# A transformer block in split fp32: the gt2 loads queued behind the up phase's high parts, and the squares of the transposed x1 taken ahead of its copy

## The chip, the cores and the metric

The kernel runs on one core of a Trainium2 chip. The metric is the time of one execution in device microseconds (us); lower is better. TensorE (PE) multiplies, PEld is its weight load, VectorE (DVE) and ScalarE (ACT) work elementwise, GpSimd (POOL) here mostly issues DMAs that add in DRAM, and SyncE (SP) issues most of the other DMAs. ACT issues DMAs too: the gt2 loads stand in its own instruction queue.

## The reference

One layer, 512 tokens, model width 2048, all in fp32. What matters here, shortened:

```python
mod = silu(c) @ w_ada + b_ada                      # (1, 6 * 2048)
sh1, sc1, gt1, sh2, sc2, gt2 = split(mod, 6)
h   = rms_norm(x, g_mix) * (1 + sc1) + sh1
mix = both head groups of h                        # recurrent and attention
x1  = x + gt1 * (mix @ w_out)
h2  = rms_norm(x1, g_ffn) * (1 + sc2) + sh2
gate, up = split(h2 @ w_up, 2)                     # 2 x 5632 columns
out = x1 + gt2 * ((silu(gate) * up) @ w_down)
```

## The kernel before

Activations lie transposed: features on the 128 partitions, 512 tokens along the row. Each fp32 operand of a matmul is split into a high part (ACT rounds a copy, `wsplit` L227) and a low part (DVE subtracts, L228), and a product is three matmuls: high by high, high by low, low by high. A framework schedules: each engine gets one queue in order, worked out at build time from priorities (`tc.high_priority(offset=...)` lifts a block) and from what depends on what. `tc.issue_after(ins)` makes every instruction of its block stand behind `ins`, if both are on the same engine. A tile pool with a tag and `bufs=n` is a ring of n buffers; a new tile waits until every reader of the old one is done.

The stages, in order: the first projections and the heads (to about 585 us), the output projection (`wo0` to `wo3`, four groups of 512 columns, 16 steps of 128 input features each), two groups of the up projection in the plain way (`up0`, `up1`), then 40 groups `uf4` to `uf43` of the up projection by a scheme of seven products of half blocks (the up phase), then the down projection in four phases (`dn`).

The six gates of `mod` are dot products of `silu(c)` with rows of `w_ada`. Five of them are computed along the way as `ada` tiles, loaded by SP. The last, gt2, is cut into 64 pieces of 128 by 512: `gt2_load(n)` loads piece n on ACT's queue into one of two buffers, `gt2_piece(n)` starts load n + 1 and has DVE multiply and sum piece n (L182). The program calls the pieces one for each chunk of the up phase, from chunk 16 on. The products end in `mods[GT2]` (`mod5`); `gt2_spread` stores it transposed to DRAM (`gt2d`, 4-byte elements, L1144) and reads it back as rows that the down projection needs at its end.

The x1 of each output group is also wanted by tokens: `x1_by_tokens(a)` has PE transpose four tiles of 128 by 128 into each of four PSUM banks, ACT copies each bank into a page in SBUF (tag "d", four pages), squares that copy into a second page with the row sums in `ss1`, and SP stores the copy as `x1t`. The banks of group a are those which group a + 2's sums take next, and `ss1` is the input of `rstd_1`, from which the up projection's operands are made (`make_t`). It is called at step 13 of the next group (`X_STEPS`), for the last group at step 6 of `up0`, and `rstd_1` is spread at step 10.

In the up phase each chunk's weights (2048 columns) give four split blocks: a, c, s and t (`uq25_1sl` is group 25, chunk 1, block s, low). The last stage's tiles are `dq4_0tl` (activations of product 4, part 0) and `dq4_0w0h` (its weights). In the profile's names such numbers are mostly left out.

Of the kernel before, what the change touches and what calls it, by code (L numbers as in the profile page):

```python
# [10 lines left out]
AF = mybir.ActivationFunctionType  # L11
# [5 lines left out]
S = 512  # L17
KT = D // P
# [13 lines left out]
SH1, SC1, GT1, SH2, SC2, GT2 = range(6)  # L32
# [27 lines left out]
def R(ap):  # L60
    return ap.bitcast(F32R)
# [3 lines left out]
def block_kernel(ctx, tc, xT, crow, adaT, vecs, bfr, w1, wyr, wqkv0, wqkv, wgate, wout, wup0, wups, wdn, outT):  # L65
    nc = tc.nc
# [15 lines left out]
    def page(name, tag, shape=None):  # L82
        return pgp.tile(shape or [P, S], F32, tag=tag, name=name, bufs=TAGS[tag])
# [85 lines left out]

    def gt2_load(n):  # L170
        t = cp.tile([P, S], F32, name=f"gt2_{n}", tag="ssq", bufs=2)
        nc.scalar.dma_start(out=t, in_=adaT[GT2 * KT + n // 4, :, (n % 4) * S:(n % 4 + 1) * S])
        gt2_src[n] = t

    def gt2_piece(n):
        if n == 0:
            gt2_load(0)
        if n < 4 * KT - 1:
            gt2_load(n + 1)
        t = gt2_src.pop(n)  # L180
        r = n % 4
        nc.vector.scalar_tensor_tensor(out=t, in0=t, scalar=1.0, in1=c_b[:, r * S:(r + 1) * S], op0=ALU.mult, op1=ALU.mult,  # L182
                                       accum_out=gt2_acc[:, r, n // 4:n // 4 + 1])
        if n == 4 * KT - 1:
            m = mods[GT2]
            nc.vector.tensor_add(m, gt2_acc[:, 0, :], vec[:, V_BADA + GT2 * KT:V_BADA + (GT2 + 1) * KT])
            for r in range(1, 4):
                nc.vector.tensor_add(m, m, gt2_acc[:, r, :])
# [4 lines left out]

    pending = []

    tail_lo = []

    def ada_some(n, ahead=True):
        with tc.issue_after(tail_lo[-1]):
# [24 lines left out]
    def wsplit(raw_ap, n, name):  # L224
        hi = wp.tile([P, 1024], F32, tag="whi", name=name + "h")
        lo = wp.tile([P, 1024], F32, tag="wlo", name=name + "l")
        nc.scalar.activation(R(hi[:, :n]), raw_ap, AF.Copy)  # L227
        tail_lo.append(nc.vector.tensor_sub(R(lo[:, :n]), raw_ap, hi[:, :n]).ins)  # L228
        return hi, lo

# [3 lines left out]
    def stream(src, kts, width, name, raw_hook=None, ahead=AHEAD):  # L234
        for q in range(len(kts) // 4):
            with tc.high_priority(offset=ahead):
                raw = wp.tile([P, 2048], F32, tag="raw", name=f"{name}r{q}", bufs=RAW)
                nc.sync.dma_start(out=raw[:, :4 * width], in_=src[kts[q * 4] // 4])
            if raw_hook:
                raw_hook(q, raw)  # L240
            for hf in range(2):
                with tc.high_priority(offset=ahead):
                    hi, lo = wsplit(raw[:, hf * 2 * width:(hf + 1) * 2 * width], 2 * width, f"{name}{q}_{hf}")
                for k2 in range(2):
                    yield kts[q * 4 + hf * 2 + k2], hi[:, k2 * width:(k2 + 1) * width], lo[:, k2 * width:(k2 + 1) * width]
# [118 lines left out]
    for kt in range(KT):  # L364
# [5 lines left out]
        a = cp.tile([P, 1], F32, name=f"A{kt}")  # L370
# [21 lines left out]
    for f in (4, 5, 6, 7, 0, 1, 2, 3):  # L392
        t = page(f"xr{f}", "c")
# [35 lines left out]
    for f in range(4):  # L429
        t = page(f"yr{f}", "c")  # L430
# [369 lines left out]
    for f in range(4):  # L800
        g, w = yr1[f], page(f"ge{4 + f}", "c")
# [23 lines left out]
    def bank(i, f, name):  # L825
        return acc(name) if i % 2 == 0 else (misc(name) if f < 3 else rgp(name))
# [20 lines left out]
    ss1 = cp.tile([P, NT, 4], F32, name="ss1")  # L847
# [3 lines left out]
    def x1_by_tokens(a):  # L851
        for t in range(NT):
            pt = bank(a + 1, t, f"x1p{a}_{t}")
            for k in range(4):
                nc.tensor.transpose(out=pt[:, k * P:(k + 1) * P], in_=x1[4 * a + k][:, t * P:(t + 1) * P], identity=ident)
            w, sq = page(f"x1w{a}_{t}", "d"), page(f"x1s{a}_{t}", "d")
            with tc.high_priority(offset=EVAC):
                nc.scalar.activation(w, pt, AF.Copy)
            nc.scalar.activation(sq, w, AF.Square, accum_out=ss1[:, t, a:a + 1])
            x1t[t, a] = drp.tile([P, S], F32, name=f"x1t{a}_{t}")  # L860
            nc.sync.dma_start(out=x1t[t, a], in_=w)
    late = []
# [5 lines left out]
    for g in range(4):  # L868
# [8 lines left out]
        if g:  # L877
            add(hk, X_STEPS[g - 1], lambda a=g - 1: x1_by_tokens(a))
        late = []
        ps = fm_group(wout[g], korder, mix, f"wo{g}", hooks=hk, ps=[bank(g + 1, f, f"wo{g}p{f}") for f in range(4)])  # L880
        for f in range(4):
            kt = g * 4 + f
            t = page(f"x1_{kt}", "c")
# [140 lines left out]
    def fast_chunk(f, c):  # L1024

        nm = f"uq{f}_{c}"
        with tc.high_priority(offset=AHEAD):
            if c:
                raw = bp.tile([P, 2048], F32, tag="raw2", name=nm + "r")
            else:  # L1030
                raw = wp.tile([P, 2048], F32, tag="raw", name=nm + "r", bufs=RAW)
            for i in range(2):
                ld = nc.sync.dma_start(out=raw[:, i * 1024:(i + 1) * 1024], in_=wups[f - 2 * STD, c, :, i * 1024:(i + 1) * 1024])
            up_loads.append(ld.ins)
            blocks = raw.rearrange("p (b m) -> p b m", b=4)
            hi, lo = wsplit(raw[:, :1024], 1024, nm + "a")
            out = [(4, hi[:, :512], lo[:, :512]), (1, hi[:, 512:], lo[:, 512:])]
            hi, lo = page(nm + "ch", "d"), page(nm + "cl", "d")
            nc.scalar.activation(R(hi), blocks[:, 3], AF.Copy)
            nc.vector.tensor_sub(R(lo), blocks[:, 3], hi)  # L1040
            out.append((2, hi, lo))
            nc.vector.tensor_add(blocks[:, 0:3:2], blocks[:, 0:2], blocks[:, 2:3].broadcast_to([P, 2, 512]))  # L1042
            nc.vector.tensor_add(blocks[:, 1], blocks[:, 1], blocks[:, 0])  # L1043
            hi, lo = wsplit(raw[:, :1024], 1024, nm + "s")
            out += [(5, hi[:, :512], lo[:, :512]), (6, hi[:, 512:], lo[:, 512:])]
            nc.vector.tensor_add(blocks[:, 3], blocks[:, 3], blocks[:, 1])  # L1046
            hi, lo = wsplit(raw[:, 1024:], 1024, nm + "t")
            out += [(7, hi[:, :512], lo[:, :512]), (3, hi[:, 512:], lo[:, 512:])]
        return out
# [5 lines left out]
    for f in range(2 * STD, FT):  # L1055
        ps = [bank(f + 1, b, f"uf{f}p{b}") for b in range(4)]
        m = {p: ps[b][:, h * HS:(h + 1) * HS] for p, (b, h) in where.items()}
        for c in range(2):
# [10 lines left out]
            n = 2 * (f - 2 * STD) + c  # L1069
# [28 lines left out]
    def dn_chunk(ph, q, hold=False):  # L1098
        prods = PHASES[ph]
        out = {p: [] for p, _, _ in prods}  # L1100
        with tc.high_priority(offset=AHEAD):
            raws, ts = [], []
            for n, (p, blk, ix) in enumerate(prods):
                nm = f"dq{p}_{q}"
                raws.append(dn_load("raw2" if n or (len(prods) == 1 and q % 2) else "raw", blk, q, nm + "r"))
                tl, th = page(nm + "tl", "h"), page(nm + "th", "h")
                nc.sync.dma_start(out=tl, in_=td[ph][q][:, ix])
                nc.scalar.activation(R(th), tl, AF.Copy)
                nc.vector.tensor_sub(R(tl), tl, th)
                ts.append((th, tl))  # L1110
            for n, (p, blk, ix) in enumerate(prods):
                nm, raw = f"dq{p}_{q}", raws[n]
                if n and blk >= 0:
                    nc.vector.tensor_add(raw, raw, raws[0])
                for k in range(2):
                    if hold and n == 0:
                        w = []
                        for i in range(2):
                            src = raw[:, (2 * k + i) * S:(2 * k + i + 1) * S]
                            hi, lo = page(f"{nm}h{k}{i}", "h"), page(f"{nm}l{k}{i}", "h")  # L1120
                            nc.scalar.activation(R(hi), src, AF.Copy)
                            nc.vector.tensor_sub(R(lo), src, hi)
                            w.append((hi, lo))
                    else:
                        hi, lo = wsplit(raw[:, k * 1024:(k + 1) * 1024], 1024, f"{nm}w{k}")
                        w = [(hi[:, i * S:(i + 1) * S], lo[:, i * S:(i + 1) * S]) for i in range(2)]
                    ks = slice(k * HS, (k + 1) * HS)
                    out[p].append((w, ts[n][0][:, ks], ts[n][1][:, ks]))
        return out
# [44 lines left out]
    for ph, prods in enumerate(PHASES):  # L1174
# [4 lines left out]
        for q in range(NQ):  # L1179
            hold = ph == 3 and q >= NQ - 2  # L1180
            out = dn_chunk(ph, q, hold)
# [101 lines left out]
```

## Time and profile before

| | |
|---|---|
| runs | 2127.1, 2125.7, 2116.4 us, median 2125.7 |
| profiled execution | 2122.55 us, its span 2120.8 us |
| granted TensorE clock, mean | 0.987 |
| busy share of PE, DVE, ACT, POOL | 97%, 81%, 45%, 4% |
| DMA | 485 MB, mean 229 GB/s |
| gt2 loads | 64 on ACT's queue, issued from 557.7 to 797.1 us |

A row of the timeline is start, length, engine, line, operation, output and inputs, and in brackets how long the engine was idle ahead of it and what ended that. `ACTq` and `SPq` are the queues' DMA issues. A group with x64 gives the shortest, median and longest duration in ns. Rows of DMA issues give the KB of one and the median us from issue to landing. The clock is the share of full speed that the throttle granted.

### The profile page before, as it was taken

How to read it: one execution, taken by the hardware profiler on the slowest of the kernel's cores; microseconds unless marked ns; L12 is line 12 of the kernel's file. 1: busy time of each engine (PE TensorE's matmuls, PEld its weight loads, DVE VectorE, ACT ScalarE, POOL GpSimd, SP SyncE). 2: the span in 40 equal slices, each digit the busy share in tenths (PEclk: the TensorE clock that was granted, in tenths of full speed). 3: DMA queues.
4: the chain of work that ended last, by engine and by line, in shares of the span. 5: the costliest groups of instructions: out<-in, count | busy, mean ns of one | idle time of the engine just before them, and what ended most of it. 6: DMA issues, size and time to landing. Idle time of an engine off the chain costs nothing.

```text
span 2120.8 us, 32408 instructions
## 1 busy us (share of the span) xinstructions
PE 2054.4 (97%) x12529; PEld 1860.5 (88%) x12529; DVE 1712.2 (81%) x2547; ACT 951.7 (45%) x1331; POOL 92.3 (4%) x111
## 2 busy tenths in 40 slices
PE   8999999999998899899999999999999999999999
PEld 6889898888776677799999999999999978888877
DVE  8999768986877577998888888888888877777785
ACT  4433447764422235444444443444444444545543
POOL 0000000000100000000000000000000000000000
PEclk9999999999998999999999999999999999999999
DMA  9989666667678754345778887777778587677784
GB/s 343 347 295 315 230 216 219 225 223 261 232 269 275 275 198 90 110 142 178 206 215 207 223 231 212 201 220 210 212 212 219 177 276 246 235 242 252 251 311 153
DMA packets 168412, 485.21 MB, mean 229 GB/s; under 512 B 20033, under 2 KB 45025, under 8 KB 163810
## 3 DMA queue, kind: packets, MB, share of 16 engines
q1 hardware_dynamic: 148898, 429.66, 59.5%
q0 software_dynamic: 10144, 36.70, 9.6%
q10 hardware_dynamic: 9216, 16.78, 2.4%
q8 instruction: 98, 1.61, 0.3%
q14 instruction: 56, 0.46, 0.1%
HBM read 447.40 MB, written 93.35 MB: 255 GB/s over the span
## 4 chain that ended last, share of the span: by engine, by line
PE 71%; DVE 13%; DMA 11%; issue 3%; ACT 1%; POOL 1%; SPq 0%; DVEq 0%; ACTq 0%
PE w1p L232 4%; DMA gt<-in_adaT 3%; PE dn7p L232 3%; PE dn1p L232 3%; PE dn5p L232 2%; PE dn6p L232 2%; PE yr1p L232 2%; PE dn4p L232 2%; PE yr0p L232 2%; PE h3p L232 2%; PE h2p L232 2%; PE h7p L232 2%; PE dn3p L232 2%; DVE ada L154 1%; PE dn2p L232 1%
## 5 line engine op out<-in xcount | busy, mean ns | idle before, releaser
L154 DVE SCALAR_TENSOR_TENSOR ada<-ada,c_b 128x1024 f32<-128x1024 f32 x96 | 115.8, 1218 | 24.4 <-DMA ada<-in_adaT 24.2
L227 ACT ACTIVATE uq_0sh<-uq_0r 128x1024 fp32r<-128x1024 f32 x40 | 42.4, 1060 | 110.8 <-DVE uq_0r L1043 110.8
L227 ACT ACTIVATE uq_1sh<-uq_1r 128x1024 fp32r<-128x1024 f32 x40 | 42.4, 1061 | 107.9 <-DVE uq_1r L1043 107.9
L228 DVE TENSOR_TENSOR uq_0al<-uq_0r,uq_0ah 128x1024 fp32r<-128x1024 f32 x40 | 49.0, 1224 | 47.3 <-ACT uq_0ah L227 45.2
L182 DVE SCALAR_TENSOR_TENSOR gt<-gt,c_b 128x512 f32<-128x512 f32 x64 | 43.0, 686 | 48.6 <-DMA gt<-in_adaT 48.3
L228 DVE TENSOR_TENSOR uq_0tl<-uq_0r,uq_0th 128x1024 fp32r<-128x1024 f32 x40 | 49.0, 1224 | 39.7 <-ACT uq_0th L227 39.7
L227 ACT ACTIVATE uq_0ah<-uq_0r 128x1024 fp32r<-128x1024 f32 x40 | 42.4, 1059 | 69.3 <-DMA td<-tw 14.5
L227 ACT ACTIVATE uq_1ah<-uq_1r 128x1024 fp32r<-128x1024 f32 x40 | 42.4, 1061 | 57.0 <-issue 57.0
L975 POOL DMA_DIRECT2D s2d<-in_wdn x44 | 36.7, 908 | 667.5 <-DMA s2d<-in_wdn 667.5
L227 ACT ACTIVATE uq_0th<-uq_0r 128x1024 fp32r<-128x1024 f32 x40 | 42.4, 1060 | 48.0 <-DVE uq_0r L1046 2.1
L228 DVE TENSOR_TENSOR uq_0sl<-uq_0r,uq_0sh 128x1024 fp32r<-128x1024 f32 x40 | 49.0, 1225 | 18.1 <-ACT uq_0sh L227 18.1
L227 ACT ACTIVATE uq_1th<-uq_1r 128x1024 fp32r<-128x1024 f32 x40 | 42.4, 1060 | 37.0 <-PE uf25p L1065 1.0
L228 DVE TENSOR_TENSOR uq_1tl<-uq_1r,uq_1th 128x1024 fp32r<-128x1024 f32 x40 | 49.0, 1224 | 10.9 <-ACT uq_1th L227 10.9
L232 PE MATMUL w1p<-hph,w1h 128*128 128x512 f32 x128 | 47.3, 398 | 4.9 <-ACT hph L376 4.9
L232 PE MATMUL w1p<-hpl,w1h 128*128 128x512 f32 x128 | 50.9, 398 | 0.0
L232 PE MATMUL w1p<-hph,w1l 128*128 128x512 f32 x128 | 50.7, 396 | 0.0
L1042 DVE TENSOR_TENSOR uq_0r<-uq_0r 128x1024 f32<-128x1024 f32 x40 | 48.7, 1218 | 0.0
L228 DVE TENSOR_TENSOR uq_1sl<-uq_1r,uq_1sh 128x1024 fp32r<-128x1024 f32 x40 | 48.6, 1215 | 0.0
L228 DVE TENSOR_TENSOR uq_1al<-uq_1r,uq_1ah 128x1024 fp32r<-128x1024 f32 x40 | 48.6, 1214 | 0.0
L1042 DVE TENSOR_TENSOR uq_1r<-uq_1r 128x1024 f32<-128x1024 f32 x40 | 48.5, 1213 | 0.0
L164 DVE SCALAR_TENSOR_TENSOR ada<-ada,c_b 128x1024 f32<-128x1024 f32 x32 | 39.0, 1217 | 1.9 <-ACT dmask_r L125 1.9
L164 DVE SCALAR_TENSOR_TENSOR adf<-adf,c_b 128x1024 f32<-128x1024 f32 x32 | 39.0, 1219 | 0.1
(12770 smaller groups left out, 8151.2 us busy)
## 6 DMA issues: line engine op xcount, KB each, us to landing
ada<-in_adaT SPq DMA_DIRECT2D x128, 512.0 KB, 5.1
uq_1r<-in_wups SPq DMA_DIRECT2D x80, 512.0 KB, 6.8
uq_0r<-in_wups SPq DMA_DIRECT2D x80, 512.0 KB, 5.0
s2d<-in_wdn POOLq DMA_DIRECT2D x44, 512.0 KB, 9.3
adf<-in_adaT SPq DMA_DIRECT2D x32, 512.0 KB, 6.0
gt<-in_adaT ACTq DMA_DIRECT2D x64, 256.0 KB, 4.6
s4d<-s2d POOLq DMA_DIRECT2D x22, 512.0 KB, 9.0
x<-in_xT SPq DMA_DIRECT2D x32, 256.0 KB, 6.2
```

What stands on the lines that cost most here:

```text
L154: nc.vector.scalar_tensor_tensor(out=t, in0=t, scalar=1.0, in1=cs, op0=ALU.mult, op1=ALU.mult, accum_out=ac)
L164: nc.vector.scalar_tensor_tensor(out=t, in0=t, scalar=1.0, in1=c_b[:, cs], op0=ALU.mult, op1=ALU.mult, accum_out=ada_acc[j][:, hf, i:i + 1])
L182: nc.vector.scalar_tensor_tensor(out=t, in0=t, scalar=1.0, in1=c_b[:, r * S:(r + 1) * S], op0=ALU.mult, op1=ALU.mult, accum_out=gt2_acc[:, ...
L227: nc.scalar.activation(R(hi[:, :n]), raw_ap, AF.Copy)
L228: tail_lo.append(nc.vector.tensor_sub(R(lo[:, :n]), raw_ap, hi[:, :n]).ins)
L232: nc.tensor.matmul(ps, lhsT=R(l), rhs=R(r), start=start, stop=stop)
L975: nc.gpsimd.dma_start(out=out[:, cs], in_=src[:, cs], accum_op=ALU.add)
L1042: nc.vector.tensor_add(blocks[:, 0:3:2], blocks[:, 0:2], blocks[:, 2:3].broadcast_to([P, 2, 512]))
```

## The change

Two edits. The gt2 loads are put behind the last high part that the program has made so far on ACT (`tail_hi`, filled in `wsplit`), wherever they are called. And `x1_by_tokens` squares the bank itself, with the square's values written into the page that the copy then overwrites, both at the copy's priority; the second page is gone.

```diff
     def gt2_load(n):
         t = cp.tile([P, S], F32, name=f"gt2_{n}", tag="ssq", bufs=2)
-        nc.scalar.dma_start(out=t, in_=adaT[GT2 * KT + n // 4, :, (n % 4) * S:(n % 4 + 1) * S])
+        with tc.issue_after(tail_hi[-1]):
+            nc.scalar.dma_start(out=t, in_=adaT[GT2 * KT + n // 4, :, (n % 4) * S:(n % 4 + 1) * S])
...
-    tail_lo = []
+    tail_lo, tail_hi = [], []
...
     def wsplit(raw_ap, n, name):
...
-        nc.scalar.activation(R(hi[:, :n]), raw_ap, AF.Copy)
+        tail_hi.append(nc.scalar.activation(R(hi[:, :n]), raw_ap, AF.Copy).ins)
...
-            w, sq = page(f"x1w{a}_{t}", "d"), page(f"x1s{a}_{t}", "d")
+            w = page(f"x1w{a}_{t}", "d")
             with tc.high_priority(offset=EVAC):
+                nc.scalar.activation(w, pt, AF.Square, accum_out=ss1[:, t, a:a + 1])
                 nc.scalar.activation(w, pt, AF.Copy)
-            nc.scalar.activation(sq, w, AF.Square, accum_out=ss1[:, t, a:a + 1])
```

Lines behind the first edit move by one. On ACT, where the first group of transposed x1 (`x1p0_0` to `x1p0_3`) is read while the second output group ends, before:

```order
L227 ACTIVATE wo20_0h_6018<-wo2r0_6016 128x1024
L172 DMA gt2_19_11794<-in_adaT 128x512
L227 ACTIVATE wo20_1h_6052<-wo2r0_6016 128x1024
L858 ACTIVATE x1w0_0_5937<-x1p0_0_5932 128x512
L172 DMA gt2_20_11905<-in_adaT 128x512
L859 ACTIVATE x1s0_0_5938,ss1_5324<-x1w0_0_5937 128x512
L858 ACTIVATE x1w0_1_5948<-x1p0_1_5943 128x512
L172 DMA gt2_21_12043<-in_adaT 128x512
L859 ACTIVATE x1s0_1_5949,ss1_5324<-x1w0_1_5948 128x512
```

The same place on ACT, after:

```order
L228 ACTIVATE wo20_0h_6014<-wo2r0_6012 128x1024
L228 ACTIVATE wo20_1h_6048<-wo2r0_6012 128x1024
L859 ACTIVATE x1w0_0_5937,ss1_5324<-x1p0_0_5932 128x512
L859 ACTIVATE x1w0_1_5947,ss1_5324<-x1p0_1_5942 128x512
L860 ACTIVATE x1w0_0_5937<-x1p0_0_5932 128x512
L860 ACTIVATE x1w0_1_5947<-x1p0_1_5942 128x512
L859 ACTIVATE x1w0_2_5957,ss1_5324<-x1p0_2_5952 128x512
L859 ACTIVATE x1w0_3_5967,ss1_5324<-x1p0_3_5962 128x512
L860 ACTIVATE x1w0_2_5957<-x1p0_2_5952 128x512
```

The loads are gone from there, and the squares stand in pairs ahead of the copies. All 64 loads now stand in the up phase: on ACT, where group 25's second chunk is split (`uw24_0`, the first read of group 24's banks, stands ahead of the first row), after:

```order
L173 DMA gt2_27_12748<-in_adaT 128x512
L228 ACTIVATE uq25_1ah_12754<-uq25_1r_12751 128x1024
L1085 ACTIVATE ug24_12626<-ug24_12626 128x512
L1040 ACTIVATE uq26_0ch_12894<-uq26_0r_12887 128x512
L228 ACTIVATE uq25_1sh_12764<-uq25_1r_12751 128x1024
L228 ACTIVATE uq25_1th_12769<-uq25_1r_12751 128x1024
L173 DMA gt2_28_12857<-in_adaT 128x512
L228 ACTIVATE uq26_0ah_12890<-uq26_0r_12887 128x1024
```

The two loads are the only rows there that are not in the kernel before. On DVE, at the end of that chunk, before:

```order
L228 TENSOR_TENSOR uq25_1sl_12781<-uq25_1r_12767,uq25_1sh_12780 128x1024
L228 TENSOR_TENSOR uq25_1tl_12786<-uq25_1r_12767,uq25_1th_12785 128x1024
L228 TENSOR_TENSOR uq26_0al_12907<-uq26_0r_12903,uq26_0ah_12906 128x1024
L1040 TENSOR_TENSOR uq26_1cl_13022<-uq26_1r_13014,uq26_1ch_13021 128x512
L1042 TENSOR_TENSOR uq26_0r_12903<-uq26_0r_12903 128x2x512
```

And on DVE at the same place, after:

```order
L229 TENSOR_TENSOR uq25_1sl_12765<-uq25_1r_12751,uq25_1sh_12764 128x1024
L183 SCALAR_TENSOR_TENSOR gt2_27_12748,gt2_acc_128<-gt2_27_12748,c_b_81 128x512
L229 TENSOR_TENSOR uq25_1tl_12770<-uq25_1r_12751,uq25_1th_12769 128x1024
L183 SCALAR_TENSOR_TENSOR gt2_28_12857,gt2_acc_128<-gt2_28_12857,c_b_81 128x512
L229 TENSOR_TENSOR uq26_0al_12891<-uq26_0r_12887,uq26_0ah_12890 128x1024
```

Two products now stand between the low parts. On SP, at the start of the down projection, the store of the finished gate stood far ahead before (behind the last `x1t` store, in `up0`); after:

```order
L1096 DMA dq5_1r_17341<-in_wdn 128x1024 x2
L1108 DMA dq5_1tl_17344<-td0_1_6718 128x512
L1145 DMA gt2d_17495<-mod5_127 128x16x1
L1154 DMA f120x_19553<-x1t0_2_5960 128x512
L1154 DMA f110x_19557<-x1t0_0_5940 128x512
L1108 DMA dq4_2tl_17417<-td0_2_6719 128x512
L1096 DMA dq4_2r_17414<-in_wdn 128x1024 x2
```

The store has moved ahead of the tiles and weights that the third step of the down projection reads.

## The prediction

> **What bounds the kernel now.** I read the profile's page first, then the time by stretches, TensorE's waits, and the timeline where those waits are longest.
>
> ```profile
> PE 2054.4 (97%) x12529; PEld 1860.5 (88%) x12529; DVE 1712.2 (81%) x2547; ACT 951.7 (45%) x1331; POOL 92.3 (4%) x111
> ```
>
> TensorE (PE) is the bound, so only what makes it wait, or slows its clock, has a price. The stretches show where that is (length, then busy us of PE, PEld, DVE, ACT, POOL; clock; DMA share; GB/s).
>
> ```profile
> 650.00:674.00 24.00, 15.58 (x46) 11.37 (x47) 18.52 (x35) 9.49 (x18) 0.00 (x0) 0.64 0.81 276
> 714.00:731.00 17.00, 12.58 (x39) 9.43 (x40) 11.36 (x24) 7.79 (x15) 0.00 (x0) 0.72 0.99 362
> 770.00:782.00 12.00, 10.54 (x38) 7.96 (x39) 9.15 (x16) 7.56 (x16) 0.00 (x0) 0.86 0.88 277
> 808.00:820.00 12.00, 10.16 (x37) 8.51 (x38) 7.04 (x12) 5.76 (x11) 1.20 (x2) 0.72 0.87 56
> 820.00:862.00 42.00, 40.94 (x185) 33.67 (x183) 41.05 (x76) 24.71 (x37) 0.00 (x0) 1.00 0.24 85
> 1300.00:1400.00 100.00, 100.00 (x835) 100.00 (x835) 83.72 (x111) 42.10 (x50) 9.93 (x12) 1.00 0.82 217
> ```
>
> In the up phase (last row) PE is full, so nothing can be won there; VectorE (DVE) has 16 us in 100 to spare. In the output projection, at 650, 714 and 770, the clock falls and PE has holes. The waits name them (us in total, times, longest).
>
> ```profile
> PE wo2p L232 <- ACT x1w L858: 9.2, 3, 3.9
> PE wo3p L232 <- ACT x1w L858: 9.1, 2, 6.8
> PE rstd_1b L305 <- POOL rstd_1t L281: 4.5, 1, 4.5
> PE up0p L232 <- ACT x1w L858: 3.8, 2, 3.4
> ```
>
> Each group needs the banks that hold the transposed x1 of an earlier group, and ScalarE (ACT) copies them out too late. The timeline of the first such place says why.
>
> ```profile
> 641.89 1.91 PE L855 MATMUL x1p<-ident,x 128*128 128x128 f32 x16
> 640.21 8.13 ACTq L172 DMA_DIRECT2D gt<-in_adaT  x3
> 646.51 0.69 DVE L182 SCALAR_TENSOR_TENSOR gt<-gt,c_b 128x512 f32<-128x512 f32 x1 [5.19 <-DMA gt<-in_adaT]
> 651.53 1.06 ACT L227 ACTIVATE wo_1h<-wo2r 128x1024 fp32r<-128x1024 f32 x1 [2.03 <-DVE gt L182]
> 652.50 0.58 ACT L858 ACTIVATE x1w<-x1p 128x512 f32<-128x512 f32 x1
> 653.13 0.80 PE L232 MATMUL wo2p<-mx8h,wo_0h 128*128 128x512 f32 x1 [3.88 <-ACT x1w L858]
> 661.74 0.63 ACT L859 ACTIVATE x1s<-x1w 128x512 f32<-128x512 f32 x1 [3.78 <-DMA x1t<-x1w]
> 662.37 0.58 ACT L858 ACTIVATE x1w<-x1p 128x512 f32<-128x512 f32 x1
> 662.45 0.34 ACTq L172 DMA_DIRECT2D gt<-in_adaT  x1
> ```
>
> The transposes are done at 643.8, but ACT's queue stands in three gt2 loads from 640.21 to 648.34: each waits for its buffer, thus for a gt2 product on DVE, thus for the load before it (5.19 us here). The first copy comes at 652.50, 8.7 us after the transposes. Then a square waits 3.78 us for a page that a store still reads, with the last bank's copy behind it.
>
> **The change, part by part.**
>
> Loads out of the output projection. All 64 gt2 loads and their products move behind high parts of the up phase. Nothing is then left between the weight splits and the copies on ACT. Its work on one group of banks is 4 x (0.63 square + 0.58 copy, by the rows above, + some 0.2 to read out the sum, an estimate) = 5.6 us. It can begin once the last split of the step, 1.06 us from 641.9, is made: 643.0 to 648.6. PE wants the first bank at 649.2 (653.13 - 3.88) and the fourth 9 matmuls, 2.0 us, later (40.94 us for 185 at full clock, 0.22 each). So all four are out in time, though two squares and a copy stand ahead of the first release instead of one copy; the margin is 2.6 us at the last. I take all three waits away: 9.2 + 9.1 + 3.8 = 22.1 us. The same waits slow the clock: PE busy times the missing clock is 15.58 x 0.36 + 12.58 x 0.28 + 10.54 x 0.14 = 10.6 us. A part of the slow clock falls on idle time, so I take 9. Ends: nothing, if ACT is as late for another reason, and 32.7.
>
> Squares first, into the copy's page. A group uses four pages of the four there are, not eight, so the wait for a store (3.78 us) has no place. At the last group the sum of squares is the input of the wait of rstd_1b; it comes sooner by more than its 4.5 us, since four PE steps (48 matmuls, 10.6 us) lie between those transposes and that use. I take 4.5. I do not take the slow clock after it (10.16 x 0.28 = 2.8): from 820 on DVE is busy for 41.05 of 42 us and sets the pace, so PE would only arrive earlier at its next wait. Ends: 0 and 7.3.
>
> What the up phase pays. Each output group (two chunks of weights, 20.16 us) gets two gt2 pieces on DVE, and two loads on ACT.
>
> ```profile
> L182 DVE SCALAR_TENSOR_TENSOR gt<-gt,c_b x64: 676/685/694, 572.1 to 800.2; 128x512 f32<-128x512 f32 x64
> gt<-in_adaT ACTq DMA_DIRECT2D x64, 256.0 KB, 4.6
> td<-ug SPq DMA_DIRECT2D x15, 256.0 KB, 5.3
> uq_1r<-in_wups SPq DMA_DIRECT2D x58, 512.0 KB, 7.4
> 1306.76 1.22 DVE L228 TENSOR_TENSOR uq_0sl<-uq_0r,uq_0sh 128x1024 fp32r<-128x1024 f32 x1 [0.48 <-ACT uq_0sh L227]
> 1312.41 0.28 PE L1065 MATMUL uf25p<-td0h,uq_0sl 128*128 128x256 f32 x1
> 1318.06 1.06 ACT L227 ACTIVATE uq_1th<-uq_1r 128x1024 fp32r<-128x1024 f32 x1 [1.01 <-PE uf25p L1065]
> 1319.15 1.23 DVE L228 TENSOR_TENSOR uq_1tl<-uq_1r,uq_1th 128x1024 fp32r<-128x1024 f32 x1 [0.60 <-ACT uq_1th L227]
> 1322.03 1.22 DVE L228 TENSOR_TENSOR uq_0al<-uq_0r,uq_0ah 128x1024 fp32r<-128x1024 f32 x1 [1.66 <-ACT uq_0ah L227]
> 1329.23 1.22 DVE L228 TENSOR_TENSOR uq_0tl<-uq_0r,uq_0th 128x1024 fp32r<-128x1024 f32 x1 [1.08 <-ACT uq_0th L227]
> 1336.15 1.06 ACT L227 ACTIVATE uq_1sh<-uq_1r 128x1024 fp32r<-128x1024 f32 x1 [2.73 <-DVE uq_1r L1043]
> 1338.22 1.06 ACT L227 ACTIVATE uq_1th<-uq_1r 128x1024 fp32r<-128x1024 f32 x1 [1.01 <-PE uf26p L1065]
> ```
>
> Busy time: 2 x 0.69 on 0.837 x 20.16 = 16.9 makes 18.3 of 20.16; it fits, and PE covers it. The latency is the danger. Of the two pieces, one is loaded half a group ahead of its product. The other's load stands right behind uq_1th on ACT, and its product right behind uq_1tl on DVE, ahead of uq_0al. A load leaves ACT as the activation ahead of it starts (662.37 and 662.45). With L from issue to landing the product starts at 1318.1 + L and uq_0al at 1318.8 + L, so it is L - 3.2 late against 1322.03. PE's smallest lead is that of uq_0sl: done at 1308.0, used at 1312.41, 4.4 us. Of a lateness, 1.1 us goes before uq_0tl, where DVE waits now. Behind it uq_1sh ends 1.0 us before uq_1th may start (1337.2 and 1338.22), so the next load goes late only if uq_0al was over 2.1 us late, L over 5.3. From there each group adds L - 5.3, and PE stands once 4.4 is reached. At 4.6, the median of these loads, PE pays nothing, and I take that, since it is the same transfer on the same queue, in a stretch as full (DMA share 0.81 at 650, 0.82 here). Ends: 0, and at 6 us 32 x 0.7 - 2.3 = 20 us.
>
> The end of the up phase. mod5, the gate that the last product completes, now goes out at the seam to the down projection, by gt2d, a store of 4-byte pieces, ahead of dq4_2tl in SP's queue.
>
> ```profile
> gt2d<-mod SPq DMA_DIRECT2D x1, 8.0 KB, 14.5
> 1687.43 0.38 SPq L1107 DMA_DIRECT2D dq_2tl<-td  x1
> 1690.89 0.63 PE L232 MATMUL dn4p<-dq_0w0h,dq_0th 128*128 128x512 f32 x2
> 1692.92 0.63 ACT L1108 ACTIVATE dq_2th<-dq_2tl 128x512 fp32r<-128x512 f32 x1 [3.77 <-DMA dq_2tl<-td]
> 1695.53 1.05 ACT L227 ACTIVATE dq_0w1h<-dq_0r 128x1024 fp32r<-128x1024 f32 x1
> 1697.72 1.21 DVE L228 TENSOR_TENSOR dq_0w1l<-dq_0r,dq_0w1h 128x1024 fp32r<-128x1024 f32 x1
> ```
>
> ACT already waits 3.77 us for dq4_2tl, and behind that stands dq5_0w1h, whose low part is ready at 1698.9, just when PE comes to it: in the new order three cells of 12 matmuls at 0.22 us, 7.9 us, behind 1690.9. If the tile lands as late as gt2d alone would (14.5 against 1692.92 - 1687.43 = 5.5), PE loses 9 and some slow clock; if the queue lets it by, nothing. I take 7: most of the way to the upper end, because tile and store share a queue.
>
> Sum, against the profiled execution's own 2122.55 us (span 2120.8, about 1.8 around it; the median of the runs is 2125.7, 3 us more): 2122.6 - 22.1 - 9 - 4.5 + 0 + 7 = 2094.0. About 0.5%, 10.6 us, is what a measurement here can tell from no change.
>
> **A rule against it.** The kernel's sums of down weights (s2d, s4d) and the weight loads run on two other queues in the up phase, and uq_1r takes 7.4 us. The Trainium skill (DMA: Bandwidth & Descriptors, Queues, rings and completion order) says that every DMA engine takes turns between the queue rows that have work, a packet at a time. By it a gt2 load that meets both gets a third of the turns, and the slower rival below is what that would give; no row of this case shows a gt2 load beside the sums.
>
> **The rivals.**
> - The up phase pays some: L near 6 because the sums are in flight for part of the time. For it: the competitor's 7.4; against it: the load goes 1.1 us ahead of uq_1r, whose issue waits for uq_1tl. 2094 + 20 = 2114.
> - Slower: L as long as uq_1r's 7.4 in every group, by sharing the engines with sums and weights. DVE is then in front of PE: 32 x 2.1 - 2.3 = 65 us, 2159. It decides from L = 6.6 on (32 x 1.3 - 2.3 = 39, enough for 2133). Against it: half the bytes of uq_1r, and 5.3 for 256 KB stores of ug in that phase.
> - Half of the gain: the squares that now stand ahead of the copies, or a late ada or wo load, hold the banks. 2094 + 31/2 = 2109.5. Against it: the margin of 2.6 us; DVE is relieved of 64 x 0.69 = 44 us there.
> - More: DVE's start from rstd_1 is free of late pages, and the seam costs nothing: 2094 - 7 - 3 = 2084.
>
> That the loads do not move is excluded by the order of the built kernel.
>
> **How the numbers follow.** Forecast 55% (2086 to 2103), half of the gain 13%, some paid 15%, slower 8%, more 9%. Below 2080 and above 2116 I leave out about 2 in 10: the slower case, the upper part of some paid, and a gain at its upper ends. Faster by over 0.5% (below 2115): the forecast, more, half, and half of some paid, 84%, less 4% where two mishaps meet, is 80%; same 7 + 4 = 11%; slower 9%.
>
> **What would show it.** Right: no wait of wo2p, wo3p or up0p for x1w, the clock at 1.0 through the output projection, no wait of rstd_1b over 1 us; the up phase at 100% PE with DVE near 91% and a DVE wait for gt of 1 to 3 us in each group; a new PE wait in dn4 or dn5 near the seam. Wrong: PE waits on uq_0sl or uq_0al in the up phase (L over 5.3), or PE still waiting for x1w.

## The result, and the profile after

| | before | after |
|---|---|---|
| median of 11 runs each | 2125.7 us | 2106.2 us |
| lowest to highest | 2116.4 to 2127.9 | 2097.1 to 2115.2 |
| ratio | | 0.9912 [0.9890, 0.9933] |
| span of the profiled execution | 2120.8 us | 2104.5 us |

The kernel became 19.5 us faster (0.9%). The forecast of 2094 lies 31.7 below the median of before; the terms of its sum, taken from the profiled execution's 2122.6, are 28.6 of that. The two profiled spans lie 16.3 us apart; the stages below are added up against that. (One execution each of two experiments, the squares alone and the first with both costs mended, took 3360 and 4071 us where the other executions of these kernels took 2114 to 2120 and 2080 to 2083; it is left out of their medians below, which with it would be 2118.2 and 2081.8.)

TensorE's waits in after, from the output projection on (us in total, times, longest):

```profile
PE dn5p L233 <- DVE ug L1080: 8.5, 1, 8.5
PE uf13p L1066 <- ACT uq_0sh L228: 3.1, 1, 3.1
...
PE dn3p L233 <- ACT dq_6w0h L228: 1.4, 1, 1.4
PE uf41p L1066 <- DVE uq_0al L229: 1.3, 1, 1.3
PE uf23p L1066 <- DVE uq_0al L229: 1.1, 1, 1.1
```

The four rows of before, for x1w and rstd_1b, are gone. In their place PE waits once at the seam (dn5p), at a few places of the up phase (uf13p, uf23p, uf41p) and near the end (dn3p).

To see what each stage gained or gave back, both traces are cut at the same early matmul of the same group (length, then busy us of PE, PEld, DVE, ACT, POOL; clock; DMA share; GB/s). Before, from wo0 to uf4, uf13 to uf43, and uf43 to dn1:

```profile
551.30:881.90 330.60, 294.46 (x1286) 239.72 (x1284) 249.48 (x446) 122.55 (x185) 7.25 (x9) 0.94 0.64 209
1067.40:1672.20 604.80, 604.80 (x5043) 604.80 (x5042) 507.34 (x660) 251.70 (x299) 46.98 (x57) 1.00 0.76 211
1672.20:1814.60 142.40, 139.96 (x686) 117.36 (x685) 112.14 (x111) 72.15 (x88) 0.00 (x0) 1.00 0.75 252
```

After, the same three:

```profile
554.20:839.90 285.70, 278.28 (x1286) 231.11 (x1285) 211.31 (x314) 120.96 (x185) 7.04 (x9) 1.00 0.54 184
1025.20:1642.40 617.20, 608.70 (x5043) 606.83 (x5042) 540.71 (x787) 246.25 (x302) 47.16 (x58) 1.00 0.81 233
1642.40:1795.10 152.70, 142.02 (x687) 118.83 (x686) 111.90 (x112) 71.04 (x86) 0.00 (x0) 0.97 0.73 233
```

The output projection with up0 and up1 takes 44.9 us less. Two things make that up: PE's idle time falls from 330.6 - 294.5 = 36.1 to 7.4 us (28.7 less), and its busy time falls by 16.2 us for the same 1286 matmuls, because the clock no longer drops. Then the up phase gives back 12.4 us, the seam (uf43 to dn1) 10.3, and the end 3.2 (from dn6 on, 186.5 us before and 189.7 after). With 2.9 us that after is late before wo0, where nothing was changed, and 0.2 in its favour between uf4 and uf13: -44.9 + 12.4 + 10.3 + 3.2 + 2.9 - 0.2 = -16.3.

The first place in the up phase where PE waits, in the timeline (start, length, engine, line, operation, output and inputs; in brackets the idle time ahead and what ended it):

```profile
1014.80 1.67 POOL L976 DMA_DIRECT2D s2d<-in_wdn  x2 [36.71 <-DMA s2d<-in_wdn]
1016.15 0.84 SPq L1034 DMA_DIRECT2D uq_1r<-in_wups  x2
1017.10 0.34 ACTq L173 DMA_DIRECT2D gt<-in_adaT  x1
1028.78 0.69 DVE L183 SCALAR_TENSOR_TENSOR gt<-gt,c_b 128x512 f32<-128x512 f32 x1 [7.89 <-DMA gt<-in_adaT]
1030.20 1.06 ACT L228 ACTIVATE uq_0sh<-uq_0r 128x1024 fp32r<-128x1024 f32 x1 [11.49 <-DVE uq_0r L1044]
```

A gt2 load leaves at 1017.1, between POOL's adding transfers and SP's weights, and lands 11.7 us later. DVE stands 7.9 us for it, with the sums of uq13_0r behind, ACT stands for those, and PE for uq_0sh. The seam shows the same kind of chain:

```profile
1655.92 0.38 SPq L1145 DMA_DIRECT2D gt2d<-mod  x1
1656.40 4.60 SPq L1154 DMA_DIRECT2D f120x<-x1t  x1
1661.80 0.41 SPq L1108 DMA_DIRECT2D dq_2tl<-td  x1
1673.77 0.63 ACT L1109 ACTIVATE dq_2th<-dq_2tl 128x512 fp32r<-128x512 f32 x1 [6.75 <-DMA dq_2tl<-td]
1674.43 0.69 DVE L1110 TENSOR_TENSOR dq_2tl<-dq_2tl,dq_2th 128x512 fp32r<-128x512 f32 x1 [6.42 <-ACT dq_2th L1109]
1675.04 0.69 DVE L1080 TENSOR_TENSOR ug<-uf43p,uw 128x512 f32<-128x512 f32 x1
1675.87 0.76 PE L233 MATMUL dn5p<-dq_0w0h,dq_0th 128*128 128x512 f32 x1 [8.47 <-DVE ug L1080]
```

gt2d goes out ahead of dq4_2tl, the tile arrives at 1673.8, DVE's low part of the tile waits for it, and the evacuation of uf43's banks, which dn5 needs, stands behind that low part on DVE. What the DMA engines did meanwhile:

```profile
1660.00:1665.00 5.00, 4.66 (x26) 3.74 (x25) 3.43 (x2) 0.00 (x0) 0.00 (x0) 1.00 0.52 14
1665.00:1670.00 5.00, 2.40 (x10) 1.60 (x9) 1.92 (x2) 1.85 (x3) 0.00 (x0) 1.00 0.60 35
1670.00:1675.00 5.00, 0.00 (x0) 0.00 (x0) 0.57 (x1) 1.23 (x2) 0.00 (x0) 0.59 0.86 280
1675.00:1680.00 5.00, 3.56 (x8) 2.41 (x9) 4.97 (x9) 2.55 (x4) 0.00 (x0) 0.50 0.51 161
```

From 1660 to 1670 they are busy for a little over half the time and move only 14 and 35 GB/s, then 280 again.

### The profile page after: what moved, and what is told of

Read it like the earlier page. It is cut to its first block, busy times and chain, and to the rows that moved or that the text cites. A ratio compares the mean times of both kernels' runs of the same rounds, so it can differ in the third digit from the quotient of the medians.

```text
span 2104.5 us, 32286 instructions
## 1 busy us (share of the span) xinstructions
PE 2046.4 (97%) x12529; PEld 1856.7 (88%) x12529; DVE 1707.3 (81%) x2547; ACT 942.3 (45%) x1331; POOL 92.2 (4%) x111
## 4 chain that ended last, share of the span: by engine, by line
PE 74%; DVE 12%; DMA 9%; issue 2%; ACT 2%; POOL 1%; SPq 0%; DVEq 0%; ACTq 0%
PE w1p L233 4%; PE dn7p L233 3%; PE dn1p L233 3%; DMA gt<-in_adaT 2%; PE dn5p L233 2%; PE dn6p L233 2%; PE yr1p L233 2%; PE up0p L233 2%; PE wo2p L233 2%; PE wo3p L233 2%; PE wo1p L233 2%; PE dn4p L233 2%; PE yr0p L233 2%; PE wo0p L233 2%; PE h3p L233 2%
## 5 line engine op out<-in xcount | busy, mean ns | idle before, releaser
L1085 ACT ACTIVATE ug<-ug 128x512 f32<-128x512 f32 x40 | 25.3, 633 | 53.5 <-DVE ug L1082 53.5
L228 ACT ACTIVATE uq_0th<-uq_0r 128x1024 fp32r<-128x1024 f32 x40 | 41.9, 1048 | 12.4 <-DVE uq_0r L1047 2.6
```

Of the source, the lines that this page charges most:

```text
L228: tail_hi.append(nc.scalar.activation(R(hi[:, :n]), raw_ap, AF.Copy).ins)
L1085: nc.scalar.activation(g, g, AF.Silu)
```

## The experiments

Each was timed against the kernel before on its own chip (medians there 2125.3 to 2125.9 us). After has a median of 2106.2.

### One half of the change at a time

Loads alone:

```diff
 # as after, with x1_by_tokens of before
-            w = page(f"x1w{a}_{t}", "d")
+            w, sq = page(f"x1w{a}_{t}", "d"), page(f"x1s{a}_{t}", "d")
...
-                nc.scalar.activation(w, pt, AF.Square, accum_out=ss1[:, t, a:a + 1])
                 nc.scalar.activation(w, pt, AF.Copy)
+            nc.scalar.activation(sq, w, AF.Square, accum_out=ss1[:, t, a:a + 1])
```

> Only the loads of gt2 are moved; the copy of the transposed x1 comes first and the squares use pages of their own, as before. Theory (both parts are needed): with no load ahead of them the copies come out in time, but a group still asks for eight pages of the four there are, so a square waits 3 to 4 us for a page that a store reads and holds up the copies behind it; part of the waits of wo2p, wo3p and up0p stays (6 to 10 us with the clock), and rstd_1b still waits some 4 us: 2110 to 2120 us, against 2106 with both parts. Rival (the loads are the whole cause): no wait of wo2p, wo3p and up0p, 2103 to 2109 us.

Squares alone:

```diff
 # as after, with gt2_load of before
-        with tc.issue_after(tail_hi[-1]):
-            nc.scalar.dma_start(out=t, in_=adaT[...])
+        nc.scalar.dma_start(out=t, in_=adaT[...])
```

> Only the squares are changed; the loads of gt2 stay where they were, in the output projection. Theory: the loads still stand ahead of the copies on ScalarE, so the waits of wo2p and wo3p stay at most of their 18 us, and what is saved is the wait of rstd_1b (4.5 us) with some clock behind it; nothing is paid in the up phase or at the seam. 2113 to 2122 us. Rival (the page of the squares was the cause): the output projection is free of waits and neither the up phase nor the seam pays, 2080 to 2086 us.

The loads alone gave 2107.5 us, 0.9907 [0.9885, 0.9930]: all of it, the rival's number, and the theory that both halves are needed fell. The squares alone gave 2116.4 us, 0.9956 [0.9939, 0.9974]. Again, for a profile:

> The same kernel as the run with only the squares changed, for a profile at full clock: 2113 to 2122 us as measured there; the waits of wo2p and wo3p for x1w are still most of 18 us, and rstd_1b waits less than before's 4.5 us.

2120.0 us in that one run. From wo0 to uf4, the loads alone, then the squares alone, then PE's largest waits there with the squares alone:

```profile
552.20:837.00 284.80, 277.48 (x1286) 230.32 (x1284) 210.89 (x313) 123.14 (x184) 6.95 (x9) 1.00 0.54 184
```

```profile
557.60:879.60 322.00, 289.37 (x1285) 236.71 (x1284) 249.30 (x446) 119.32 (x184) 7.24 (x9) 0.96 0.65 215
```

```profile
PE wo3p L232 <- ACT x1w L859: 5.8, 1, 5.8
PE wo2p L232 <- ACT x1w L859: 4.7, 1, 4.7
PE up0p L232 <- ACT x1w L859: 3.8, 1, 3.8
```

The loads on ACT are the cause. With them away the stage takes 284.8 us with the old squares and 285.7 with the new. With them in place the new squares take out the wait of rstd_1b and a part of the others: x1w is still 14.3 of 22.1 us. PE's idle time in the stage falls by only 3.5 us (36.1 to 32.6), because its waits for the split weights (wo_0h, wo_0l) grow from 0.8 to 8.5 us. The two gains do not add up (18.4 and 9.5 against 19.5 together): what the squares can save, the loads' move saves already.

### What the up phase pays

Products later: a load had some 10 us to land, instead of the 1 to 6 of the even ones (gt2_0, gt2_2 and so on: load right behind uq_1th on ACT, product right behind uq_1tl on DVE).

```diff
-        nc.vector.scalar_tensor_tensor(out=t, in0=t, ...)
+        with tc.issue_after(tail_lo[-1]):
+            nc.vector.scalar_tensor_tensor(out=t, in0=t, ...)
```

> As after, but each product of gt2 on VectorE is put behind the low part t of its own chunk, so that a load has some 10 us to land before VectorE wants it, instead of the 1 to 6 us that the even ones had; the number of products and loads is the same. Theory (the landing time of the even pieces is what the up phase pays): the waits of VectorE for gt fall from 60 us to under 10, those of uf13p, uf17p, uf23p and uf41p on uq_0s and uq_0a go, and the time is 10 to 13 us less: 2093 to 2097 us. Rival (the up phase pays for VectorE's 44 us of added work, or for weights that land late beside the added loads): the waits only change their place, 2103 to 2109 us.

2092.8 us, 0.9843 [0.9826, 0.9859], with all runs from 2091.5 to 2093.7. Its up phase (uf13 to uf43) and DVE's waits for gt in it, then the same waits in after:

```profile
1025.60:1630.40 604.80, 604.80 (x5042) 604.80 (x5041) 538.19 (x781) 254.98 (x300) 46.96 (x57) 1.00 0.82 238
```

```profile
DVE gt L184 <- DMA gt<-in_adaT: 1.7, 1, 1.7
```

```profile
DVE gt L183 <- DMA gt<-in_adaT: 60.5, 20, 7.9
```

The stage is back at 604.8 us to the digit, with the same products on DVE: its added work costs nothing. The loads don't land sooner (median 4.9, longest 11.3 us); they are wanted later. The four runs lie within 2.2 us, where the 11 of after spread over 18; that the landing times make this scatter isn't shown, since before spreads over 12 without them.

Why a load takes that long:

```diff
 def dram_sum(out, src):
...
-            nc.gpsimd.dma_start(out=out[:, cs], in_=src[:, cs], accum_op=ALU.add)
+            pass
```

> As after, but the four adding transfers on GpSimd's queue that make each s2d and s4d are left out (the plain copies into s2d and s4d on SP's queue stay, so the down projection computes with weights that aren't summed). Theory (a gt2 load lands late because it shares the DMA engines with these transfers): the waits of VectorE for gt fall from 60 us to under 25, uf13p no longer waits, and the up phase pays 0 to 4 us instead of 12: 2093 to 2099 us. Rival (the landing time comes from the weight loads and the stores of the transformed ug, which run on SP's queue beside the loads): the waits for gt stay over 40 us and the time is 2102 to 2108 us.

2093.9 us, 0.9852 [0.9829, 0.9875]. The up phase takes 604.8 us here too. Landing of a gt2 load (shortest, median, longest), after and then without the adding transfers, and DVE's waits without them:

```profile
DMA to landing us min/median/max: 2.4/4.7/11.7
```

```profile
DMA to landing us min/median/max: 2.4/2.7/6.9
```

```profile
DVE gt L183 <- DMA gt<-in_adaT: 28.4, 17, 3.7
```

The waits of DVE halve (28.4 us, just over the 25 expected) and none is longer than 3.7, which PE's lead covers. So it is the adding transfers beside which a gt2 load lands late; weights and stores on SP's queue alone are not enough. The DMA share falls too, from 0.81 to 0.55, so this run can't tell the adding from the mere traffic.

### What the seam pays

gt2d on another queue:

```diff
-        nc.sync.dma_start(out=gd.rearrange("k p -> p k"), in_=mods[GT2])
+        for k in range(0, KT, 4):
+            nc.gpsimd.dma_start(out=gd[k:k + 4].rearrange("k p -> p k"), in_=mods[GT2][:, k:k + 4])
```

> As after, but gt2d, the store of 4-byte pieces at the seam, goes out on GpSimd's queue in four pieces, so that no tile of the down projection stands behind it on SP's. Theory (the store blocks SP's queue): dq_1tl and dq_2tl land in 4 to 6 us, the wait of 8.5 us of dn5p goes, and the time is 10 us less: 2094 to 2099 us. Rival (the 2048 pieces load the DMA engines whatever the queue, or the low part is late for another reason): a wait of 5 to 9 us stays in dn4p or dn5p, 2102 to 2108 us.

2113.8 us, 0.9940 [0.9922, 0.9958]: 6 (by the ratios) to 8 us slower than after, outside both expectations. The stage uf43 to dn1 grows to 164.9 us. PE's longest waits there, then the landing of SP's tiles and of gt2d (KB of one, median us):

```profile
PE dn5p L233 <- DVE dq_2w0l L229: 7.0, 1, 7.0
PE dn5p L233 <- DVE ug L1080: 4.0, 1, 4.0
```

```profile
dq_2tl<-td SPq DMA_DIRECT2D x2, 256.0 KB, 14.0
dq_3tl<-td SPq DMA_DIRECT2D x2, 256.0 KB, 14.9
...
gt2d<-mod POOLq DMA_DIRECT2D x4, 2.0 KB, 12.5
```

With the store on POOL's queue, tiles on SP's land after 14 us and more. So the delay doesn't come from standing behind the store on one queue. The 14 and 35 GB/s of the whole core, while the store is under way in after, point at something that all queues share; what it is isn't shown. That the cost rose can't be put down to the queue, because the cut into four changed more: the parts left one behind another, at 1657.7, 1670.3, 1682.2 and 1695.9 us, and each took some 12.5 us to land, so the store lasted some 50 us instead of 14.1. The profiled execution was also the slowest of its six (2119.2 us).

No store of 4-byte pieces at all (PE turns mod5, and rows are stored in the third phase of the down projection), with the products as in after:

```diff
+        pt = bank(2, 0, "gt2t")
+        nc.tensor.transpose(out=pt[:KT, :P], in_=mods[GT2], identity=ident)
+        row = page("gt2row", "c")
+        nc.vector.tensor_copy(out=row[:KT, :P], in_=pt[:KT, :P])
-        nc.sync.dma_start(out=gd.rearrange("k p -> p k"), in_=mods[GT2])
+        nc.sync.dma_start(out=gd, in_=row[:KT, :P])
...
-            if ph == 0 and q == 2:
+            if ph == 2 and q == 2:
                 gt2_spread()
```

> As after, with mod5 turned by TensorE and stored as rows of 512 bytes in the third phase of the down projection, and the products left where the change put them. Theory (seam and up phase pay apart from each other): the seam's 10 us go and the up phase's 12 stay: 2093 to 2099 us, with the up phase's waits of VectorE for gt still near 60 us. Rival (the late tiles at the seam come from what the up phase left late): 2102 to 2108 us.

2098.4 us, 0.9871 [0.9849, 0.9892]. Its up phase and its seam, in the profiled execution (2106.0 us, the slowest of its four):

```profile
1029.00:1652.90 623.90, 612.33 (x5043) 609.98 (x5042) 541.17 (x787) 246.10 (x302) 47.55 (x58) 0.99 0.80 230
1652.90:1794.70 141.80, 139.58 (x687) 117.49 (x686) 112.34 (x113) 71.47 (x87) 0.00 (x0) 1.00 0.73 246
```

The seam is at 141.8 us (before: 142.4), while the up phase pays 19.1 us in this execution. So the two costs are separate. The rows land in 5.3 us, and the core's DMA moves 258 GB/s in the 5 us from 1932, when they are stored. Form and place were changed together: rows at the seam were not run, nor 4-byte pieces in the third phase.

The store as it was, elsewhere: with the products later, and gt2d held back on SP's queue behind the loads of chunk 4 of the second down phase (`issue_after` on that load).

> The products put behind the low part t of their own chunk (2092.8 us by itself), and the store gt2d, still of 4-byte pieces, held back on SP's queue until the second phase of the down projection, behind the load of its chunk 4. Theory (the store holds the DMA engines for 12 us wherever it goes): the seam's 10 us go, and dn1p or dn7p waits 4 to 12 us at the new place: 2085 to 2092 us. Rival (only the seam is sensitive, where the outputs of uf43 and the first tiles are queued behind each other; within a phase the loads are a chunk ahead): no new wait over 2 us, 2080 to 2084 us.

2087.4 us, 0.9816 [0.9792, 0.9840]. From uf43 to dn1, and from dn1 to dn6, where the store now is:

```profile
1633.70:1774.50 140.80, 139.53 (x687) 117.46 (x686) 113.55 (x117) 72.33 (x88) 0.00 (x0) 1.00 0.73 249
1774.50:1900.10 125.60, 122.05 (x529) 99.84 (x528) 89.15 (x77) 60.16 (x72) 0.00 (x0) 0.99 0.76 239
```

The seam is cured, and the new place pays: 125.6 us against 119.6 in the run below that has no such store there. That is 6 us instead of 10, of which 3.6 are idle and the rest slow clock; the seam is the dearer place, but not the only one.

### Both mended

The products later and gt2d as rows:

> The products put behind the low part t of their own chunk (2092.8 us by itself), and with that mod5 turned by TensorE in the third phase of the down projection and stored as 16 rows of 512 bytes, so that there is no store of 4-byte pieces at the seam. Theory (that store, on whatever queue, holds the DMA engines for 12 us while tiles and weights of the seam are wanted): dn5p's wait for ug, 10 us, goes; at most 3 us of waits stay in dn4p and dn5p as before the change, and the time is 10 to 13 us less: 2080 to 2084 us. Rival (the stall comes from the order of tiles and splits at the seam, with the store beside it by chance): a wait of 5 to 10 us stays, 2088 to 2093 us.

2081.4 us, 0.9792 [0.9769, 0.9815]. Again, for a profile:

> The version at 2081.8 us again, for a profile at full clock: 2080 to 2084 us, TensorE at 100% from wo1 to the seam but for bup_p and up1p, no wait of dn4p or dn5p over 3 us.

2079.4 us, 0.9784 [0.9758, 0.9811]. Its stages uf43 to dn1 and dn1 to dn6, and all of PE's waits of 1 us or more from wo0 to the end:

```profile
1630.80:1770.90 140.10, 139.19 (x687) 117.60 (x686) 113.16 (x117) 71.87 (x88) 0.00 (x0) 1.00 0.74 251
1770.90:1890.50 119.60, 119.60 (x529) 99.06 (x528) 89.60 (x77) 61.19 (x72) 0.00 (x0) 1.00 0.71 242
```

```profile
PE bup_p L1002 <- DVE bu_acc L947: 2.7, 1, 2.7
PE up1p L234 <- ACT up_0h L229: 2.6, 1, 2.6
PE ratiob L307 <- POOL ratiot L302: 1.4, 1, 1.4
PE dn2p L234 <- DVE dq_5w1l L230: 1.0, 1, 1.0
```

And the same with the squares as they were before the change:

> The version at 2081.8 us (products behind their own chunk, mod5 stored as rows), with the copy first and the squares in pages of their own, as before the change. Theory (with the loads out of the output projection the order of the squares is worth nothing, as in the run with the loads alone): no wait of wo2p, wo3p, up0p for x1w and none of rstd_1b over 1 us, 2079 to 2084 us. Rival (the pages still cost something that the scatter of the earlier run hid): 2086 to 2091 us.

2078.1 us, 0.9780 [0.9758, 0.9802], 47 us faster than before and 28 faster than after. Its interval overlaps that of the version with the new squares, so the order of the squares is worth nothing that these runs can tell. From wo0 to uf4 it takes 284.9 us, where the loads alone took 284.8.

## Why the prediction was right, and where its sizes were off

The forecast was 2094 in a range of 2080 to 2116, faster with 0.80. It came to 2106.2: faster, in the range, and between the forecast and the rival "the up phase pays some" (2114). What that rival describes (L near 6 while the adding transfers are in flight) is what happened, at 12.4 us instead of its 20. Part of the nearness is luck: 15.6 us at the up phase and the end, which the sum had at 0, were about half made up by 7.2 us of clock that it had not counted on.

**Waits of the output projection: right.** 22.1 + 4.5 = 26.6 us were taken away in the sum; idle time fell by 28.7. The margin of 2.6 us held.

**The clock: 9 in the sum, 16.2 measured.** The wide rows show that PE's busy time fell from 294.5 to 278.3. The prediction's three windows held all the slow clock of their waits (from one to the next the clock is at 0.99 to 1.00), 10.6 us, and 1.6 of it was taken off without need. The 2.8 us behind rstd_1b were left out with the reason that DVE sets the pace there; in after PE is busy for all of the 40 us from 780 to 820, so DVE does not hold it. And the last 20 us ahead of uf4 were not counted: the clock is 0.88 there before and 0.95 after, worth 1.2 us of PE's 15.8 and 14.8. That makes 14.6 of the 16.2; the rest is open. A slow clock outlasts its wait, as at the seam in after: 0.59 from 1670 to 1675, and 0.50 in the 5 us behind, with PE at work again from 1675.9. The Trainium skill (TensorE: Matmul & The Clock Gate, Part 1) says that the clock falls to half after an idle window of about 3.4 us and comes back after a busy one; the trace agrees in kind, and the window itself wasn't measured here.

**Squares first: 4.5 given to it, 0 measured.** rstd_1b's wait did go, but with the loads alone it went too. The step took a wait that both halves of the change remove and put it down to one.

**The up phase: 0 in the sum, 12.4 measured.** The rule of it was right: the lateness of the even pieces, a few us of PE's lead, and a cost from a landing time over 5.3. What failed is the landing time that it was fed with: 4.6 us is the median of loads beside which no adding transfer ran (before's last load leaves at 797.1, its first adding transfer at 996.1). In after only even pieces are waited for, 20 of the 32, and, counted load by load, these are just the ones with an adding transfer in flight. 17 of them have a landing time in the trace: 5.6 to 11.7 us, all over the 5.3. Of the other 12 even pieces 11 have one, 2.6 to 4.3, and DVE waits for none of the 12. The median of all 64 loads, 4.7, comes near the 4.6 only because it mixes both kinds with the odd pieces, which have half a group more. One even piece of each kind, the first beside adding transfers that leave at 1160.1, 1164.7 and 1169.6:

```profile
1162.70 0.33 ACTq L173 DMA_DIRECT2D gt<-in_adaT  x1
1170.77 0.69 DVE L183 SCALAR_TENSOR_TENSOR gt<-gt,c_b 128x512 f32<-128x512 f32 x1 [4.76 <-DMA gt<-in_adaT]
1185.30 0.34 ACTq L173 DMA_DIRECT2D gt<-in_adaT  x1
1189.91 0.68 DVE L183 SCALAR_TENSOR_TENSOR gt<-gt,c_b 128x512 f32<-128x512 f32 x1
```

Every third group has no adding transfer beside its even piece, and DVE does not wait there. So the lateness does not grow from group to group through the phase, as the rival's 20 us had it, and PE loses time in five groups only: 5.8 us at uf13 (it starts at 1025.2 and uf14 at 1051.2, where a group takes 20.2) and 0.5 to 2.1 at uf17, uf20, uf23 and uf41. The trace of before had a warning, a longest landing of 8.9 us, that the sum didn't use (landing of its gt2 loads, shortest, median, longest):

```profile
DMA to landing us min/median/max: 2.5/4.6/8.9
```

The reason given for 4.6, "in a stretch as full", compared DMA shares, not which transfers make them up. The rule of the Trainium skill that the prediction named against itself (DMA: Bandwidth & Descriptors, Queues, rings and completion order: an engine takes turns between its queue rows) fits the run without the adding transfers, median 4.7 to 2.7 us, but no run here shows the turns themselves: less traffic of any kind might do the same. And the loads are not late in every group, as the slower rival had it: 12 of the 32 even pieces meet no adding transfer.

**The seam: 7 in the sum, 10.3 measured.** The place, the tile (dq4_2tl) and the cause (gt2d) were right. Two things were not. The reason given for the size, that tile and store share a queue, fell: with the store on another queue the tiles landed no sooner. And what stood behind the tile was not dq5_0w1h but the evacuation of uf43's banks on DVE.

**The end: 3.2 us not forecast.** dn3p waits 1.4 us for dq_6w0h and the clock drops a little. The wait is 0.7 us with the products later, 0.8 with rows, 1.2 without the adding transfers, and gone with both costs mended. In nine profiles of the experiments the stage takes 186.3 to 189.9 us, so a part of the 3.2 may be no more than that scatter. The cause stays open.

By its own terms the sum would have been 2122.6 - 28.7 - 16.2 + 12.4 + 10.3 + 3.2 + 2.9 - 0.2 = 2106.3, the span of 2104.5 and the 1.8 around it.

## What to carry to other kernels

When a transfer is moved, look at which other transfers are in flight at each place where it is used, and compare the time it has there with the landing time of loads that meet the same company, not with the median of loads from another place. A load that can't be made shorter can often be given more time for nothing: here its user went behind the work of its own chunk, which won back all 12 us. A small store of tiny pieces is not small: moved within the down projection, it brought its cost along (10 us at the seam, 6 in the second phase). As rows, and in the third phase, it cost nothing that these runs show.

## What the hardware showed that was not expected

- 8 KB in 2048 pieces of 4 bytes (gt2d) took 11.4 to 14.5 us to land in the runs, and in after the whole core's DMA moved 14 to 35 GB/s for some 10 us of that. In four parts on POOL's queue each part of 2 KB took 12.5 us in the median, and tiles of 256 KB on SP's queue took 14.0 and 14.9 us meanwhile, against 4.4 to 5.8 for dq_0tl to dq_4tl in before, without the store.
- While it was in progress two of SP's own issues of loads took 4.60 and 5.11 us instead of some 0.4.
- A 256 KB load on ACT's queue landed in 5.6 to 11.7 us beside transfers that add in DRAM on POOL's (17 even pieces of after), and in 2.6 to 4.3 without them (11), in a stage with a DMA share of 0.81.
